# The order of the high and the low product in feature-major column tiles of a hybrid encoder block

## The chip, the cores and the metric

The kernel runs on one core of a Trainium2 chip. The metric is device time in microseconds (us) of one execution, lower is better. Engines are called as in the profile: PE (TensorE, its weight loads apart as PEld), DVE (VectorE), ACT (ScalarE), POOL (GpSimd), SP (which issues most of the DMAs).

## What is computed

One residual block over 256 tokens of width 2048, in float32: an RMS norm, one wide projection (`w_in`), stick-breaking attention with 16 heads and a Mamba-2 scan with 8 groups side by side, their gated sum through `w_out`, then a GeGLU MLP with a depthwise convolution ahead of the activation. Cut to what matters:

```python
h = rms_norm(x, norm_mix_pre)
q, k, v, z, xbc, dt, g_sb, g_ssd = jnp.split(h @ w_in, cuts, axis=-1)
o_sb = stick_breaking_attention(q, k, v)
xbc = silu(causal_dwconv(xbc, ssd_conv_w, ssd_conv_b))      # -> xs, bm, cm
y = ssd_scan(xs, softplus(dt + dt_bias), -exp(a_log), bm, cm)
y = rms_norm((y + xs * d_skip) * silu(z), ssd_norm)
x = x + rms_norm((sigmoid(g_sb) * (o_sb @ w_sb_proj) + sigmoid(g_ssd) * (y @ w_ssd_proj)) @ w_out, ...)
u = causal_dwconv(rms_norm(x, norm_ffn_pre) @ w_up, ffn_conv_w, ffn_conv_b)
x = x + rms_norm((gelu(gate) * val) @ w_down, norm_ffn_post)
```

Every large matrix product is made from three products of rounded halves: each float32 operand is split into a high half (`hi`, rounded to the fp32r type) and a low half (`lo`, the rest), and hi·hi, lo·hi and hi·lo are summed.

## The kernel before

**Weights.** All weights stream from HBM once, as 715 units of 128x1024. SP loads a unit into `raw` (5 buffers); `prep` splits it: ACT casts `whi` from `raw` (L63) and DVE subtracts `wlo` from both (L64), 5 buffers each. `unit()` (L95) hands out the next unit and keeps the splitting three units ahead.

**Two kinds of column tiles.** In token-major tiles (`tok_mm`, L136) activations are the weights of PE and each step is three products of 512 columns, `ps_z`, `ps_ssd`, `ps_fo` and others. In feature-major tiles a 128-wide column of the weight matrix is PE's stationary operand, and the activation chunk `act[:, k, :, :]` holds the high half of 256 tokens and then the low half. So one weight tile k of 16 needs two products into one PSUM bank `ps` of 512 columns: the high weights over both halves (512 columns, L112), and the low weights over the high half (256 columns, into the first 256 columns, L113). `feat_mm` (L115) runs 16 weight tiles for one bank, which is two units; `feat_mms` (L123) does the same for four or two banks side by side, four weight tiles at a time, where activations arrive late. Feature-major are `ps_first` (start), `ps_xs` and `ps_bc` (scan inputs, 6 tiles for each of 8 groups), `ps_qk` (32 tiles) and the up projection `ps_fg` and `ps_fv` (43 tiles each, after the first pair `ps_f0`).

**Taking a bank out.** `feat_sum` copies the second half of the bank with ACT (L133), and DVE adds the first half (L134). A convolution follows: for the scan `conv_silu` (DVE L314, ACT L315, three DVE steps L317, ACT's silu L318), for the MLP `conv3`.

**The scan of a group.** `ssd_work` is a generator whose steps `pump()` puts between PE's large products, during `ps_z` of the group and the next group's `ps_xs`: eight transposes `px` (L332), DVE's `xw` from them (L333), copies by ACT (L334), scalings by POOL (L336, L335), the decay matrix `mm` by DVE (L338), masked by POOL (L339), ACT's exponential (L347) and a copy of `pcb` to `xw` (L345), and then the product `po` (L353), which needs that copy.

**What sets the order.** Most of the order on each engine comes from a scheduler that places instructions when the program is built, by its own estimate of when their inputs are ready; only the first stage, the norm after `w_out` and the end are written out by hand (`manual_schedule`). So a change in when a bank counts as finished can move ACT's and DVE's instructions too.

Of the kernel before, what the change touches and what calls it, by code (L numbers as in the profile page):

```python
# [17 lines left out]
P = 128  # L18
T = 256
KT = 16  # L20
# [18 lines left out]
def block_kernel(ctx, tc, xT, xN, wts, vecs, rows, hvec, dskip, gain, out):  # L39


    nc = tc.nc
# [38 lines left out]
    def prep(parts=1):  # L81

        v = state["u"]
        state["u"] += 1
        if v not in raw_t:
            load(v)
        raw = raw_t.pop(v)
        hi = wspl.tile([P, 1024], F32R, tag="whi", name=f"whi{v}")
        lo = wspl.tile([P, 1024], F32R, tag="wlo", name=f"wlo{v}")
        spl_t[v] = (hi, lo)  # L90
        n = 1024 // parts
        for i in range(parts):
            w = slice(i * n, (i + 1) * n)
            split(hi[:, w], lo[:, w], raw[:, w])
            yield  # L95

    def unit(ahead=WBUFS - 2):

        u = state["at"]
        state["at"] += 1  # L100
        while state["u"] <= min(u + ahead, n_units - 1):
            for _ in prep():
                pass
        return spl_t.pop(u)

    def mm_bank(name):
        return pmm.tile([P, 512], F32, tag="mm", name=name)

    def feat_tile(ps, hi, lo, c, act, k, last):

        w = slice(c * P, (c + 1) * P)
        nc.tensor.matmul(ps, hi[:, w], act[:, k % 4, :, :].rearrange("p s t -> p (s t)"), start=(k == 0), stop=last)  # L112
        nc.tensor.matmul(ps[:, :T], lo[:, w], act[:, k % 4, 0, :], start=False, stop=last, skip_group_check=True)  # L113

    def feat_mm(acts, name):  # L115
        ps = mm_bank(name)
        for k in range(KT):
            if k % 8 == 0:
                hi, lo = unit()
            feat_tile(ps, hi, lo, k % 8, acts[k // 4], k, k == KT - 1)  # L120
        return ps

    def feat_mms(acts, pss):  # L123

        for kc in range(4):
            for i, ps in enumerate(pss):
                if i % 2 == 0:
                    hi, lo = unit()
                for k in range(4):
                    feat_tile(ps, hi, lo, 4 * (i % 2) + k, acts[kc], 4 * kc + k, 4 * kc + k == KT - 1)  # L130

    def feat_sum(ps, dst):
        nc.scalar.copy(dst, ps[:, T:])  # L133
# [2 lines left out]
    def tok_mm(acts, nk, name):  # L136

        pss = [mm_bank(f"{name}_{t}") for t in range(2)]
        for k in range(nk):
            if k % 2 == 0:  # L140
                hi, lo = unit()
            w = slice(k % 2 * 512, k % 2 * 512 + 512)
            for t in range(2):
                ah, al = (acts[k // 4][:, k % 4, s, t * P:(t + 1) * P] for s in range(2))
                nc.tensor.matmul(pss[t], ah, hi[:, w], start=(k == 0), stop=False)  # L145
                nc.tensor.matmul(pss[t], ah, lo[:, w], start=False, stop=False)  # L146
                nc.tensor.matmul(pss[t], al, hi[:, w], start=False, stop=(k == nk - 1))  # L147
            if k % 4 == 3:
                pump()
        return pss  # L150
# [155 lines left out]
    def conv_in(ps, ti):  # L306
        raw = tmp.tile([P, T], F32, tag="cv_raw", name=f"cvr{ti}", bufs=3)
        feat_sum(ps, raw)
        return raw
# [91 lines left out]
    first = [mm_bank(f"ps_first{i}") for i in range(3)]  # L401
    first.append(paux.tile([P, 512], F32, tag="aux", name="ps_first3"))
    feat_mms(a_ch, first)
    feat_sum(first[0][:64, :], dts[:64, 0, :])
    first = [None] + [conv_in(first[i], i - 1) for i in range(1, 4)]
    stats_x()
    for g in range(GROUPS):
        xf = []
        for j in range(4):
            xf.append(tmp.tile([P, T], F32, tag=f"xf{j}", name=f"xf{g}_{j}", bufs=1))  # L410
            if g == 0 and j < 3:
                continue
            ps = feat_mm(a_ch, f"ps_xs{g}_{j}")
            if g == 0:
                tok_to_bc(rstd_bc, rstd_tok, paux, "aux", "rx")
                bg.append(dt_work())
                for i in range(3):
                    conv_silu(first[i + 1], i, xf[i])
            conv_silu(conv_in(ps, 4 * g + j), 4 * g + j, xf[j])
            pump()  # L420
        bcs = []
        for j in range(2):
            ps = feat_mm(a_ch, f"ps_bc{g}_{j}")
            bcs.append(tmp.tile([P, T], F32, tag=f"bc{j}", name=f"bc{g}_{j}", bufs=1))
            conv_silu(conv_in(ps, 32 + 8 * j + g), 32 + 8 * j + g, bcs[j])
            pump()
        drain()
        csb = slot(F32, [8, T], f"csb{g}")
        nc.gpsimd.dma_start(csb, cs_dram[8 * g:8 * g + 8, :].partition_broadcast(P))
        xs = slot(F32, [2, 2, 512], f"xs{g}")  # L430
        bg.append(ssd_work(g, xf, bcs[0], bcs[1], xs, csb))
        pz = tok_mm(a_ch, KT, f"ps_z{g}")
        for t in range(2):
            nc.scalar.activation(xs[:, 0, t, :], pz[t], AF.Silu, scale=rstd_tok[:, t:t + 1])
# [12 lines left out]
    for n in range(4):  # L447
        ps = tok_mm(y_ch, 32, f"ps_ssd{n}")
# [69 lines left out]
    for hg in range(4):  # L518
        qk = slot(F32, [2, 4, T], f"qk{hg}")
        for i in range(2):  # L520
            for h in range(4):
                ps = feat_mm(a_ch, f"ps_qk{hg}_{i}_{h}")
                d = qk[:, i, h, :]
                feat_sum(ps, d)
                nc.vector.scalar_tensor_tensor(d, d, SCALE if i == 0 else 1.0, rstd_bc, op0=ALU.mult, op1=ALU.mult)
                pump()
        vt = slot(F32, [2, 512], f"v{hg}")
        pv = tok_mm(a_ch, KT, f"ps_v{hg}")
        for t in range(2):
            nc.scalar.activation(vt[:, t, :], pv[t], AF.Copy, scale=rstd_tok[:, t:t + 1])  # L530
        bg.append(attn_work(hg, qk, vt))
# [15 lines left out]
    for n in range(4):  # L547
        ps = tok_mm(o_ch, KT, f"ps_sb{n}")
# [59 lines left out]
    for n in range(4):  # L608
        ps = tok_mm(m_ch, KT, f"ps_mo{n}")
# [9 lines left out]
    with tc.manual_schedule(engines=ACT_DVE):  # L619
# [8 lines left out]
        for i in range(8 + lag):  # L628
            if i < 8:
                n, t = divmod(i, 2)  # L630
# [3 lines left out]
            if i >= lag:  # L634
                n, t = divmod(i - lag, 2)
# [43 lines left out]
    for j in range(FF_T):  # L679
        if j == 0:  # L680
            first = [mm_bank(f"ps_f0_{i}") for i in range(2)]
            feat_mms(h_ch, first)
            continue
        pg = feat_mm(h_ch, f"ps_fg{j}")
        pv = feat_mm(h_ch, f"ps_fv{j}")
        if j == 1:
            for t in range(2):
                nc.gpsimd.dma_start(x2_dram[t], xn[t])
            tok_to_bc(r2, n2.r, paux, "tp", "r2")
            ffn_out(0, *first)  # L690
        ffn_out(j, pg, pv)
# [11 lines left out]
    for n in range(4):  # L703
        gfo = tmp.tile([P, 512], F32, tag="gfo", name=f"gfo{n}")
        nc.gpsimd.dma_start(gfo, rows[2, blk(n)].partition_broadcast(P))
        ps = tok_mm(f_ch, FF_T, f"ps_fo{n}")
# [6 lines left out]
    with tc.manual_schedule(engines=ACT_DVE):  # L713
# [6 lines left out]
        for n in range(4):  # L720
            for t in range(2):
                parts = 2 if n == 3 and t == 1 else 1
                for i in range(parts):
                    w = slice(n * 512 + i * 256, (n + 1) * 512 - (parts - 1 - i) * 256)
# [84 lines left out]
```

## Time and profile before

| | |
|---|---|
| median of 3 runs | 2100.11 us (2099.76 to 2102.88) |
| the profiled execution | 2101.31 us |
| span of its trace | 2099.6 us |
| PE busy | 2072.1 us, 99% |
| weight loads (beside PE) | 1760.7 us, 84% |
| DVE / ACT / POOL busy | 1386.0 / 1156.9 / 152.3 us |
| DMA | 402.79 MB, mean 192 GB/s |

The span runs from the first to the last instruction in the trace; the time of the execution holds it and a little around it. PE is busy in all but a few places. A busy PE is not a PE at its peak: how long a product really holds PE is read from the distance of two starts, since a product's recorded length runs into the next one.

### The profile page before, as it was taken

How to read it: one execution, taken by the hardware profiler on the slowest of the kernel's cores; microseconds unless marked ns; L12 is line 12 of the kernel's file. 1: busy time of each engine (PE TensorE's matmuls, PEld its weight loads, DVE VectorE, ACT ScalarE, POOL GpSimd, SP SyncE). 2: the span in 40 equal slices, each digit the busy share in tenths (PEclk: the TensorE clock that was granted, in tenths of full speed). 3: DMA queues.
4: the chain of work that ended last, by engine and by line, in shares of the span. 5: the costliest groups of instructions: out<-in, count | busy, mean ns of one | idle time of the engine just before them, and what ended most of it. 6: DMA issues, size and time to landing. Idle time of an engine off the chain costs nothing.

```text
span 2099.6 us, 27950 instructions
## 1 busy us (share of the span) xinstructions
PE 2072.1 (99%) x10632; PEld 1760.7 (84%) x10632; DVE 1386.0 (66%) x1794; ACT 1156.9 (55%) x1542; POOL 152.3 (7%) x134
## 2 busy tenths in 40 slices
PE   9999999999999999999999999999999999999997
PEld 7788888888888888888888888788888888888886
DVE  6888877788544445555544566598878887854443
ACT  6767677667543334555556444475555555544442
POOL 0222102222000000000000021100000000000000
PEclk9999999999999999999999999999999999999999
DMA  8564565555555555555555746475555555565653
GB/s 297 194 205 160 190 205 186 176 199 179 187 197 192 192 194 186 180 171 171 170 172 185 274 161 210 141 250 191 189 190 190 189 189 190 191 232 202 195 193 109
DMA packets 109094, 402.79 MB, mean 192 GB/s; under 512 B 12416, under 2 KB 12672, under 8 KB 106656
## 3 DMA queue, kind: packets, MB, share of 16 engines
q1 hardware_dynamic: 104912, 380.07, 54.1%
q0 software_dynamic: 3328, 20.02, 2.7%
q8 instruction: 83, 1.36, 0.3%
q10 hardware_dynamic: 720, 0.93, 0.1%
q14 instruction: 51, 0.42, 0.1%
HBM read 396.71 MB, written 4.26 MB: 191 GB/s over the span
## 4 chain that ended last, share of the span: by engine, by line
PE 92%; POOL 2%; DVE 2%; issue 2%; DMA 1%; ACT 1%; SPq 0%; DVEq 0%; ACTq 0%; POOLq 0%
PE ps_fv L112 8%; PE ps_fg L112 8%; PE ps_qk L112 6%; PE ps_xs L112 5%; PE ps_fo L147 4%; PE ps_fo L145 4%; PE ps_fo L146 4%; PE ps_fg L113 4%; PE ps_fv L113 4%; PE ps_qk L113 3%; PE ps_ssd L147 3%; PE ps_ssd L145 3%; PE ps_ssd L146 3%; PE ps_xs L113 2%; PE ps_bc L112 2%; PE ps_z L146 2%
## 5 line engine op out<-in xcount | busy, mean ns | idle before, releaser
L64 DVE TENSOR_TENSOR wlo<-raw,whi 128x1024 fp32r<-128x1024 f32 (+1 forms) x715 | 905.1, 1270 | 601.2 <-ACT whi L63 600.6
L63 ACT CAST whi<-raw 128x1024 fp32r<-128x1024 f32 (+1 forms) x715 | 746.2, 1051 | 793.7 <-PE ps_fo L147 128.9
L112 PE MATMUL ps_fg<-h,whi 128*128 128x512 f32 x688 | 240.7, 394 | 0.0
L112 PE MATMUL ps_fv<-h,whi 128*128 128x512 f32 x688 | 240.6, 394 | 0.0
L113 PE MATMUL ps_fg<-h,wlo 128*128 128x256 f32 x688 | 190.6, 277 | 0.0
L113 PE MATMUL ps_fv<-h,wlo 128*128 128x256 f32 x688 | 190.6, 277 | 0.0
L112 PE MATMUL ps_qk<-a,whi 128*128 128x512 f32 x512 | 181.3, 398 | 0.0
L112 PE MATMUL ps_xs<-a,whi 128*128 128x512 f32 x464 | 162.9, 396 | 0.0
L112 PEld LDWEIGHTS ps_fv<-h,whi 128*128 128x128 f32 x688 | 129.0, 188 | 30.0
L112 PEld LDWEIGHTS ps_fg<-h,whi 128*128 128x128 f32 x688 | 129.0, 188 | 30.0
L113 PE MATMUL ps_qk<-a,wlo 128*128 128x256 f32 x512 | 143.5, 280 | 0.0
L145 PE MATMUL ps_fo<-whi,f 128*128 128x512 f32 x352 | 136.9, 389 | 0.0
L147 PE MATMUL ps_fo<-whi,f 128*128 128x512 f32 x352 | 136.9, 389 | 0.0
L146 PE MATMUL ps_fo<-wlo,f 128*128 128x512 f32 x352 | 136.9, 389 | 0.0
L113 PEld LDWEIGHTS ps_fg<-h,wlo 128*128 128x128 f32 x688 | 129.2, 188 | 0.0
L113 PEld LDWEIGHTS ps_fv<-h,wlo 128*128 128x128 f32 x688 | 129.2, 188 | 0.0
L113 PE MATMUL ps_xs<-a,wlo 128*128 128x256 f32 x464 | 129.0, 278 | 0.0
L112 PEld LDWEIGHTS ps_qk<-a,whi 128*128 128x128 f32 x512 | 96.1, 188 | 22.6
L145 PE MATMUL ps_z<-whi,a 128*128 128x512 f32 x256 | 103.7, 407 | 0.0
L112 PEld LDWEIGHTS ps_xs<-a,whi 128*128 128x128 f32 x464 | 87.1, 188 | 19.6
L146 PE MATMUL ps_z<-wlo,a 128*128 128x512 f32 x256 | 100.4, 392 | 1.0 <-DVE wlo L64 1.0
L147 PE MATMUL ps_z<-whi,a 128*128 128x512 f32 x256 | 100.1, 391 | 0.0
(282 smaller groups left out, 3832.5 us busy)
## 6 DMA issues: line engine op xcount, KB each, us to landing
raw<-wts SPq DMA_DIRECT2D x713, 512.0 KB, 3.8
csb<-cs_dram POOLq DMA_DIRECT2D x8, 1024.0 KB, 8.1
xt<-xN SPq DMA_DIRECT2D x2, 1024.0 KB, 10.6
csb<-gain POOLq DMA_DIRECT2D x8, 256.0 KB, 4.1
xn<-xN POOLq DMA_DIRECT2D x2, 1024.0 KB, 7.9
x_dram<-xn POOLq DMA_DIRECT2D x2, 1024.0 KB, 9.0
xe<-x_dram POOLq DMA_DIRECT2D x2, 1024.0 KB, 10.3
x<-xT SPq DMA_DIRECT2D x3, 512.0 KB, 9.2
```

What stands on the lines that cost most here:

```text
L63: nc.scalar.copy(hi, src)
L64: nc.vector.tensor_tensor(lo, src, hi.bitcast(F32), op=ALU.subtract)
L112: nc.tensor.matmul(ps, hi[:, w], act[:, k % 4, :, :].rearrange("p s t -> p (s t)"), start=(k == 0), stop=last)
L113: nc.tensor.matmul(ps[:, :T], lo[:, w], act[:, k % 4, 0, :], start=False, stop=last, skip_group_check=True)
L145: nc.tensor.matmul(pss[t], ah, hi[:, w], start=(k == 0), stop=False)
L146: nc.tensor.matmul(pss[t], ah, lo[:, w], start=False, stop=False)
L147: nc.tensor.matmul(pss[t], al, hi[:, w], start=False, stop=(k == nk - 1))
```

## The change

`feat_tile` and the loops around it are replaced by `feat_run`. It goes through a run of weight tiles (16 in `feat_mm`, 4 in `feat_mms`). In the first weight tile of a run the 512-column product with the high half still comes first; from the second on the 256-column product with the low half comes ahead of the 512-column product. So a run that was hi lo, hi lo, hi lo, ... is now hi lo, lo hi, lo hi, ..., and ends on a 512-column product. Number, size and operands of the products are the same.

```diff
-    def feat_tile(ps, hi, lo, c, act, k, last):
-        w = slice(c * P, (c + 1) * P)
-        nc.tensor.matmul(ps, hi[:, w], act[:, k % 4, :, :].rearrange("p s t -> p (s t)"), start=(k == 0), stop=last)
-        nc.tensor.matmul(ps[:, :T], lo[:, w], act[:, k % 4, 0, :], start=False, stop=last, skip_group_check=True)
+    def feat_run(ps, act, tiles, n, first, last):
+        for i, (hi, lo, k) in enumerate(tiles):
+            a = act(k)
+            for part in ("hi", "lo") if i == 0 else ("lo", "hi"):
+                end = last and i == n - 1
+                if part == "hi":
+                    nc.tensor.matmul(ps, hi, a.rearrange("p s t -> p (s t)"), start=first and i == 0, stop=end)
+                else:
+                    nc.tensor.matmul(ps[:, :T], lo, a[:, 0, :], start=False, stop=end, skip_group_check=True)
...
     def feat_mm(acts, name):
...
-            feat_tile(ps, hi, lo, k % 8, acts[k // 4], k, k == KT - 1)
+        feat_run(ps, lambda k: acts[k // 4][:, k % 4, :, :], tiles(), KT, True, True)
...
     def feat_mms(acts, pss):
...
-                for k in range(4):
-                    feat_tile(ps, hi, lo, 4 * (i % 2) + k, acts[kc], 4 * kc + k, 4 * kc + k == KT - 1)
+                feat_run(ps, lambda k: acts[kc][:, k, :, :], [(*w_tile(w, 4 * (i % 2) + k), k) for k in range(4)], 4, kc == 0, kc == 3)
```

The line numbers of the changed file are 5 to 12 higher: the two products are L117 and L119 there, `feat_sum` is L145 and L146, and later lines are 12 higher. In the rows of order below, numbers behind a name are buffer numbers.

PE, the beginning of the column tile `ps_fg41` of the up projection, before:

```order
L113 MATMUL ps_fv40_15637<-h3_11052,wlo613_15596 128x256
...
L112 MATMUL ps_fg41_15703<-h0_11049,whi614_15617 128x512
L113 MATMUL ps_fg41_15703<-h0_11049,wlo614_15618 128x256
L112 MATMUL ps_fg41_15703<-h0_11049,whi614_15617 128x512
L113 MATMUL ps_fg41_15703<-h0_11049,wlo614_15618 128x256
```

and now:

```order
L117 MATMUL ps_fv40_15637<-h3_11052,whi613_15595 128x512
...
L117 MATMUL ps_fg41_15703<-h0_11049,whi614_15617 128x512
L119 MATMUL ps_fg41_15703<-h0_11049,wlo614_15618 128x256 x2
L117 MATMUL ps_fg41_15703<-h0_11049,whi614_15617 128x512
L119 MATMUL ps_fg41_15703<-h0_11049,wlo614_15618 128x256
```

Two 256-column products now stand together at each beginning, and two 512-column products at each boundary between tiles. Everything else on PE, the transposes and products of the scan and of attention among them, has kept its place in the row.

DVE, in group 2 of the scan, from the bank of the group's last feature-major tile (`ps_bc2_1`, taken out to `cvr42`) to `xw2`, before:

```order
L64 TENSOR_TENSOR wlo58_1823<-raw58_1820,whi58_1822 128x1024
L134 TENSOR_TENSOR cvr42_1787<-cvr42_1787,ps_bc2_1_1741 128x256
L314 TENSOR_TENSOR cvr42_1787<-cvr42_1787,rstd_bc_218 128x256
L64 TENSOR_TENSOR wlo59_1868<-raw59_1865,whi59_1867 128x1024
L317 SCALAR_TENSOR_TENSOR cva42_1790<-cvr42_1787,vec_93,cva42_1790 128x255
L317 SCALAR_TENSOR_TENSOR cva42_1790<-cvr42_1787,vec_93,cva42_1790 128x254
L317 SCALAR_TENSOR_TENSOR cva42_1790<-cvr42_1787,vec_93,cva42_1790 128x253
L333 TENSOR_TENSOR xw2_1838<-px2_0_1840,dt_tok_220 128x512
```

and now:

```order
L146 TENSOR_TENSOR cvr42_1787<-cvr42_1787,ps_bc2_1_1741 128x256
L326 TENSOR_TENSOR cvr42_1787<-cvr42_1787,rstd_bc_218 128x256
L64 TENSOR_TENSOR wlo58_1823<-raw58_1820,whi58_1822 128x1024
L329 SCALAR_TENSOR_TENSOR cva42_1790<-cvr42_1787,vec_93,cva42_1790 128x255
L329 SCALAR_TENSOR_TENSOR cva42_1790<-cvr42_1787,vec_93,cva42_1790 128x254
L329 SCALAR_TENSOR_TENSOR cva42_1790<-cvr42_1787,vec_93,cva42_1790 128x253
L64 TENSOR_TENSOR wlo59_1868<-raw59_1865,whi59_1867 128x1024
L345 TENSOR_TENSOR xw2_1838<-px2_0_1840,dt_tok_220 128x512
```

The taking out of the bank and its convolution now stand one weight unit earlier than before. Groups 3 to 7 show the same pair of orders; group 1 had the second order before the change, and keeps it.

ACT at the same place, before:

```order
L63 CAST whi58_1822<-raw58_1820 128x1024
L318 ACTIVATE bc2_0_1730<-cva34_1734 128x256
L133 COPY cvr42_1787<-ps_bc2_1_1741 128x256
L63 CAST whi59_1867<-raw59_1865 128x1024
L315 ACTIVATE cva42_1790<-cvr42_1787,vec_93 128x256
L63 CAST whi60_1885<-raw60_1883 128x1024
L318 ACTIVATE bc2_1_1786<-cva42_1790 128x256
L334 COPY xs2_1799<-px2_0_1840 128x512
```

and now:

```order
L330 ACTIVATE bc2_0_1730<-cva34_1734 128x256
L145 COPY cvr42_1787<-ps_bc2_1_1741 128x256
L63 CAST whi58_1822<-raw58_1820 128x1024
L327 ACTIVATE cva42_1790<-cvr42_1787,vec_93 128x256
L63 CAST whi59_1867<-raw59_1865 128x1024
L330 ACTIVATE bc2_1_1786<-cva42_1790 128x256
L63 CAST whi60_1885<-raw60_1883 128x1024
L346 COPY xs2_1799<-px2_0_1840 128x512
```

Here too the convolution's steps stand one weight cast earlier. ACT's list also has 18 fewer table loads (63 instead of 81), three for each of the groups 1 to 6, in the stage of the next group's `ps_xs`.

DVE in group 0, after `rstd_bc` (the reciprocal norm, which all convolutions of the scan need), before:

```order
L254 COPY rstd_bc_218<-rx_ps_449 128x256
L64 TENSOR_TENSOR wlo14_533<-raw14_530,whi14_532 128x1024
L314 TENSOR_TENSOR cvr0_379<-cvr0_379,rstd_bc_218 128x256
...
L317 SCALAR_TENSOR_TENSOR cva1_461<-cvr1_382,vec_93,cva1_461 128x253
L264 TENSOR_SCALAR dts_226<-dts_226,hv_195 64x256
L64 TENSOR_TENSOR wlo15_567<-raw15_564,whi15_566 128x1024
L317 SCALAR_TENSOR_TENSOR cva2_468<-cvr2_385,vec_93,cva2_468 128x255
```

and now:

```order
L266 COPY rstd_bc_218<-rx_ps_449 128x256
L326 TENSOR_TENSOR cvr0_379<-cvr0_379,rstd_bc_218 128x256
...
L329 SCALAR_TENSOR_TENSOR cva1_461<-cvr1_382,vec_93,cva1_461 128x253
L276 TENSOR_SCALAR dts_226<-dts_226,hv_195 64x256
L64 TENSOR_TENSOR wlo14_533<-raw14_530,whi14_532 128x1024
L64 TENSOR_TENSOR wlo15_567<-raw15_564,whi15_566 128x1024
L329 SCALAR_TENSOR_TENSOR cva2_468<-cvr2_385,vec_93,cva2_468 128x255
```

The split of unit 14 has moved behind the eleven instructions that follow `rstd_bc`. SP's and POOL's lists, the DMAs among them, are the same as before.

## Rows read from the trace of the kernel before

**Rows 1.** The page: the span, and busy time, share of the span and instructions of each engine.

```profile
span 2099.6 us, 27950 instructions
...
PE 2072.1 (99%) x10632; PEld 1760.7 (84%) x10632; DVE 1386.0 (66%) x1794; ACT 1156.9 (55%) x1542; POOL 152.3 (7%) x134
```

**Rows 2.** The waits of PE, the five longest of eight: who waited, for whom, us in total, times, the longest.

```profile
PE po L353 <- ACT xw L345: 3.7, 6, 0.7
PE pth L385 <- DVE mog L632: 2.9, 1, 2.9
PE ps_first L112 <- DVE a L197: 2.9, 2, 2.1
PE po L353 <- POOL xw L336: 2.4, 1, 2.4
...
PE ps_z L146 <- DVE wlo L64: 1.0, 1, 1.0
```

**Rows 3.** PE in order of time in the up projection, across the boundary of two column tiles: start, recorded length, instruction.

```profile
1502.74 0.39 PE L112 MATMUL ps_fv<-h,whi 128*128 128x512 f32 x1
...
1503.32 0.28 PE L113 MATMUL ps_fv<-h,wlo 128*128 128x256 f32 x1
1503.44 0.39 PE L112 MATMUL ps_fg<-h,whi 128*128 128x512 f32 x1
...
1503.78 0.40 PE L112 MATMUL ps_fg<-h,whi 128*128 128x512 f32 x1
```

**Rows 4.** PE in order of time in the first `ps_qk` tiles; between the two rows stand two other pairs.

```profile
805.17 0.40 PE L112 MATMUL ps_qk<-a,whi 128*128 128x512 f32 x1
...
806.23 0.40 PE L112 MATMUL ps_qk<-a,whi 128*128 128x512 f32 x1
```

**Rows 5.** The page's costliest groups: two of the 512-column products, with count, busy time and mean ns of one.

```profile
L112 PE MATMUL ps_fg<-h,whi 128*128 128x512 f32 x688 | 240.7, 394 | 0.0
...
L112 PE MATMUL ps_qk<-a,whi 128*128 128x512 f32 x512 | 181.3, 398 | 0.0
```

**Rows 6.** Group 1 of the scan, during its `ps_z`, in order of time, of PE, then DVE, then POOL: start, length, instruction, and the idle time before it with what ended it.

```profile
126.19 1.04 PE L332 MATMUL px<-ident,xf 128*128 128x128 f32 x8
...
138.92 0.67 PE L353 MATMUL po<-xw 128*128 128x512 f32 x1
...
125.06 1.22 DVE L64 TENSOR_TENSOR wlo<-raw,whi 128x1024 fp32r<-128x1024 f32 x1
126.83 1.29 DVE L333 TENSOR_TENSOR xw<-px,dt_tok 128x512 f32<-128x512 f32 x2 [0.55 <-PE px L332]
...
127.61 1.03 POOL L336 TENSOR_TENSOR xw<-xw,dec 128x512 f32<-128x512 f32 x1 [39.58 <-DVE xw L333]
```

**Rows 7.** Group 2 at the same place, of PE, DVE, ACT and POOL.

```profile
188.57 1.04 PE L332 MATMUL px<-ident,xf 128*128 128x128 f32 x8
...
201.79 0.67 PE L353 MATMUL po<-xw 128*128 128x512 f32 x1 [0.60 <-ACT xw L345]
...
187.13 1.23 DVE L64 TENSOR_TENSOR wlo<-raw,whi 128x1024 fp32r<-128x1024 f32 x1 [0.69 <-ACT whi L63]
188.27 1.52 DVE L317 SCALAR_TENSOR_TENSOR cva<-cvr,vec,cva 128x255 f32<-128x255 f32 x3
189.70 1.28 DVE L333 TENSOR_TENSOR xw<-px,dt_tok 128x512 f32<-128x512 f32 x2
...
188.77 1.05 ACT L63 CAST whi<-raw 128x1024 fp32r<-128x1024 f32 x1 [1.18 <-PE ps_z L147]
...
190.42 1.19 ACT L334 COPY xs<-px 128x512 f32<-128x512 f32 x2
...
190.48 1.03 POOL L336 TENSOR_TENSOR xw<-xw,dec 128x512 f32<-128x512 f32 x1 [43.58 <-DVE xw L333]
```

**Rows 8.** Group 7 at the same place, PE alone; groups 3 to 6 stand between.

```profile
502.90 1.04 PE L332 MATMUL px<-ident,xf 128*128 128x128 f32 x8
...
516.12 0.67 PE L353 MATMUL po<-xw 128*128 128x512 f32 x1 [0.59 <-ACT xw L345]
```

**Rows 9.** Group 0, from `rstd_bc` to the wait in `ps_z`: one row of PE, then DVE, then ACT, in order of time.

```profile
58.73 0.50 PE L146 MATMUL ps_z<-wlo,a 128*128 128x512 f32 x1 [1.00 <-DVE wlo L64]
...
41.28 1.23 DVE L64 TENSOR_TENSOR wlo<-raw,whi 128x1024 fp32r<-128x1024 f32 x1
42.42 1.09 DVE L314 TENSOR_TENSOR cvr<-cvr,rstd_bc 128x256 f32<-128x256 f32 x3
...
46.39 1.21 DVE L64 TENSOR_TENSOR wlo<-raw,whi 128x1024 fp32r<-128x1024 f32 x1
48.43 0.48 DVE L317 SCALAR_TENSOR_TENSOR cva<-cvr,vec,cva 128x255 f32<-128x255 f32 x1 [0.84 <-ACT cva L315]
...
57.46 1.22 DVE L64 TENSOR_TENSOR wlo<-raw,whi 128x1024 fp32r<-128x1024 f32 x1
...
45.89 1.28 ACT L318 ACT_TABLE_LOAD   x1 [0.97 <-DVE cva L317]
...
47.81 0.59 ACT L315 ACTIVATE cva<-cvr,vec 128x256 f32<-128x256 f32 x1
```

**Rows 10.** Busy time of each engine in two stretches, with PE's granted clock as a share of full speed (after POOL).

```profile
9.00:15.20 6.20, 5.25 (x16) 4.48 (x17) 4.79 (x9) 5.41 (x10) 0.00 (x0) 0.50 1.03 417
1353.50:1357.00 3.50, 3.46 (x19) 3.21 (x17) 3.50 (x7) 2.27 (x4) 0.00 (x0) 0.51 0.00 0
```

More of the change, by code (lines that the diff above doesn't have):

```diff
@@ L107, in mm_bank, with w_tile, tiles @@
         return pmm.tile([P, 512], F32, tag="mm", name=name)
-    def feat_tile(ps, hi, lo, c, act, k, last):
-        w = slice(c * P, (c + 1) * P)
-        nc.tensor.matmul(ps, hi[:, w], act[:, k % 4, :, :].rearrange("p s t -> p (s t)"), start=(k == 0), stop=last)
-        nc.tensor.matmul(ps[:, :T], lo[:, w], act[:, k % 4, 0, :], start=False, stop=last, skip_group_check=True)
+    def feat_run(ps, act, tiles, n, first, last):
[7 more added lines that the diff above has]
+                    nc.tensor.matmul(ps[:, :T], lo, a[:, 0, :], start=False, stop=end, skip_group_check=True)
+    def w_tile(w, c):
+        return tuple(x[:, c * P:(c + 1) * P] for x in w)
     def feat_mm(acts, name):
         ps = mm_bank(name)
-        for k in range(KT):
-            if k % 8 == 0:
-                hi, lo = unit()
-            feat_tile(ps, hi, lo, k % 8, acts[k // 4], k, k == KT - 1)
+        def tiles():
+            for k in range(KT):
+                if k % 8 == 0:
+                    w = unit()
+                yield *w_tile(w, k % 8), k
+        feat_run(ps, lambda k: acts[k // 4][:, k % 4, :, :], tiles(), KT, True, True)
         return ps
@@ L127, in feat_mms @@
                 if i % 2 == 0:
-                    hi, lo = unit()
-                for k in range(4):
-                    feat_tile(ps, hi, lo, 4 * (i % 2) + k, acts[kc], 4 * kc + k, 4 * kc + k == KT - 1)
+                    w = unit()
+                feat_run(ps, lambda k: acts[kc][:, k, :, :], [(*w_tile(w, 4 * (i % 2) + k), k) for k in range(4)], 4, kc == 0, kc == 3)
     def feat_sum(ps, dst):
```

## The prediction

> **What bounds the kernel now.** I read the page's busy shares first, then PE's waits, then PE in order of time, then DVE and ACT around each wait. PE is busy for 2072.1 of 2099.6 us and DVE, the next engine, for 66% [rows 1]. So the time moves in two ways only: by how fast PE goes through its row of products, or by places where PE stands still.
>
> For the rate, the distance of starts counts. In the up projection three pairs of a 512- and a 256-column product take 1503.78 - 1502.74 = 1.04 us, 0.347 us a pair, and the tile boundary that lies inside (`ps_fv` to `ps_fg`) adds nothing [rows 3]. In the first `ps_qk` tiles three pairs of the same shape take 1.06 us, 0.353 us a pair [rows 4]; the page's mean lengths of the 512-column product, 394 and 398 ns, differ in the same direction [rows 5]. So identical instructions run in two rhythms 1.06 - 1.04 = 0.02 us per three pairs apart, that is 6.7 ns a pair (a difference of rounded rows, good to some ns). Each lasts through whole stages.
>
> PE's listed waits are few, and three bear on the change: `po` on ACT's copy 3.7 us in six pieces, `po` on POOL 2.4 us once, `ps_z` on DVE's `wlo` 1.0 us once [rows 2]. The two others in that list lie at the start and between attention and the gate, on norm and gate steps whose row the change leaves alone.
>
> **Part 1, the products.** Removed and added: nothing. There are (43 + 43) x 16 = 1376 pairs in the up projection (688 of them `ps_fg` [rows 5]), 512 in `ps_qk`, 48 x 16 = 768 in the scan's inputs, and some 64 more at the start and in the first up pair, 2720 in all. Each run of 16 keeps 16 products of either size. After each product stands another that needs new weights, before and now; what is new are two neighbours of a kind at each end of a run (256 after 256, 512 after 512). If a product holds PE for its columns and a fixed share, the sum of a run is the same, whatever the order: 0. No row of before shows 256 after 256 in this form, so the cost is bounded by the nearest rows, the two rhythms: from -6.7 ns to +6.7 ns a pair, where a stage could still change over. I take 0, because rows 3 are nearest: there a boundary, where 256 follows 512 and another bank begins, costs nothing that can be read. Weights: the low half is now wanted 0.23 us or so earlier in a run (second, instead of fourth, in line at the second weight tile), but no wait of a feature-major product on `wlo` is in the list [rows 2], and splitting is three units ahead, so 0.
>
> How the trace bears on a rule here: the 1.04 us for three pairs stay above the pure columns, 3 x 768 / 2.4 = 960 ns [rows 3], at the higher of the clock's two levels. The Trainium skill ("TensorE: Matmul & The Clock Gate", Part 2, Back-to-back issue gap) gives N/2.4 + 2.5 ns a product, by which a pair is an estimated 325 ns in any order, and its Part 2, Step-by-step, says that weight loads do not take bandwidth from a running product. By it no order of neighbours could cost anything, and both rivals on the rhythm would be void; rows 3 and 4, at 347 and 353 ns for the same instructions, do not agree with one fixed figure, so the measurement decides and these rivals keep their chances.
>
> **Part 2, a bank's end.** The last product of a bank is now the one of 512 columns, which writes both halves, where ACT could before start on the second half while the 256-column product ran (by its columns 256 / 2.4 = 107 ns; with its share of the overhead about 0.12 us). So ACT's copy comes 0.12 us later, at each of 163 or so banks. I cost that at nothing: `px` needs `xf` only after the group's last tiles, `ps_z` covers it, and the up projection's convolutions are a tile behind. If this cover were gone everywhere it would be 163 x 0.12 = 19.6 us. The `whi` buffer comes free 0.12 us later too, once per unit, with four more behind it. ACT's 18 dropped table loads (1.28 us each [rows 9]) free ACT, which is at 55% [rows 1]: 0 on the path. SP's and POOL's rows are the same, so no DMA moves in its queue.
>
> **Part 3, groups 2 to 7 of the scan.** This is where PE stands still. In group 1 `px` starts at 126.19 and `po` at 138.92, 12.73 us later, with no wait written at it [rows 6]; in group 2 it is 201.79 - 188.57 = 13.22, with 0.60 of wait on ACT's copy [rows 7]; in group 7 516.12 - 502.90 = 13.22, with 0.59 [rows 8]. PE's row is the same in all of them, so the 0.49 is lost time. Back along the chain: ACT's copy stands behind the exponential of the matrix that POOL masks, and POOL does that after its `xw`; POOL starts 127.61 in group 1 and 190.48 in group 2, and from there to `po` it is 11.31 us in both (138.92 - 127.61, 201.79 - 190.48). So the delay arises ahead of POOL, and passes on one for one. DVE makes `xw` from `px`: in group 1 at 126.83, 0.64 after `px`, having waited for PE [rows 6]; in group 2 at 189.70, 1.13 after `px`, because three steps L317 of the last convolution, from 188.27, still stand ahead and run until 189.79 [rows 7]. 1.13 - 0.64 = 0.49 again.
>
> The change gives groups 2 to 7 the order that group 1 had: L314 and L317 of the last convolution stand one weight split earlier on DVE, and on ACT the copies and L315 one cast earlier (ACT's cast at 188.77, after an idle 1.18, stands between them [rows 7]). What is moved behind, the split of a later unit (1.23 us), is wanted three units on. So I expect 0.49 x 6 = 2.94 us less. Bounds: 0, if something else is late instead (DVE's split of 1.22 us, which in group 1 stands directly ahead of `xw` at 125.06 and ends 0.55 before it [rows 6]), and 3.7, all the wait of the row [rows 2]. I take 2.9 to 3.0, because group 1 shows the very order. Next late after it is `px` itself, that is PE.
>
> **Part 4, group 0.** After `rstd_bc` DVE splits unit 14 first (41.28, 1.23 us), then does L314 and what follows at 42.42 [rows 9]. Now the split goes behind eleven instructions, so these start 1.14 us earlier. ACT's table load at 45.89, which waited 0.97 for DVE's L317, comes at 44.75; behind it `cva` (47.81 + 0.59) ends at 47.26 instead of 48.40. DVE will do split 14 at about 45.25 and split 15 at 46.39 as before, until about 47.5; so its idle 0.84 before 48.43 [rows 9] goes, and its dense list after it starts about 0.9 us earlier. Split 14 is wanted only by `ps_z` of group 0, some 4 us after its new end. In that list stands split 16 (57.46), on which PE waits 1.00 at 58.73 [rows 9]; 0.9 to 1.0 of it goes. The rest of group 0's chain (`px`, POOL, the 2.4 us wait of `po` [rows 2]) hangs on the same list and moves with it, not more than PE does. I take -1.0; bounds 0 (something else on the list takes the time) and -1.16 (1.14 moved, with rounding).
>
> **The sum.** 0 + 0 - 3.0 - 1.0 = -4.0 us. Against the profiled execution, 2101.31 - 4.0 = 2097.3; the median of the three runs, 2100.11, is 1.2 below that execution, so **2096.1 us** (-0.19%). From run to run about 0.2%, 4.2 us, can be told from no change, so the forecast stands just at that line (2095.9).
>
> One thing can shift all cases: the granted clock. It stands at 0.50 for a stretch at the start (9.0 to 15.2) and 0.51 at 1353.5 to 1357.0 [rows 10], that is the lower level; at half speed 3.5 us of PE's work holds 1.75 us of loss, and a stretch that begins or ends elsewhere could bring or take so much.
>
> **The rivals.**
>
> *A: no gain.* The wait comes back elsewhere: PE reaches the next gate, the exponential or POOL, as much earlier as it saved, and waits there, or the mended order loses its lead to a later cast. Then 2100.1. For it: `po` of group 0 waits for POOL anyway [rows 2]. Against it: group 1 has no wait with this order [rows 6].
>
> *B: slower.* The up projection loses its rhythm. Its 1376 pairs are in the quicker one now [rows 3]; what sets a rhythm is not in the rows, but it seems to be taken on entry into a stage and kept, so a boundary with two equal neighbours, which comes 86 times, may throw it into the other. Price: 1376 x 6.7 ns = 9.2 us, so 2096.1 + 9.2 = 2105.3, or +5.2 on the time before (+0.25%). It decides against the forecast as soon as more than 4.0 / 0.0067, some 600 pairs, go over, and is past the measurable from about 1230. For it: two rhythms exist, with the same instructions [rows 3, 4]. Against it: old boundaries also change bank and weights, and leave the rhythm alone.
>
> *C: more gain.* The same, with the other sign: `ps_qk`'s 512 pairs fall into the quicker rhythm: 512 x 6.7 ns = 3.4 us, 2092.7.
>
> *D: the change does not do what it says.* Each run could still be built with the low product behind. The built order shows it in front; this has no chance left worth a number.
>
> **How the numbers follow.** Forecast 0.57, with 2094.3 to 2097.6 as its own range (gains of 5.8 to 2.5: the bounds of parts 3 and 4, and the clock); half of it lies past 2095.9. A 0.15, same. B 0.14, of which 0.12 beyond 2104.3 and 0.02 in between. C 0.14, faster. So faster 0.27 + 0.14 = 0.41, same 0.30 + 0.15 + 0.02 = 0.47, slower 0.12. For 8 in 10 the range holds the forecast and A whole, and C down to 2092.3; it leaves out B's full price and a few hundredths at the ends: 2092.3 to 2101.0.
>
> **What would show it.** Right: `px` to `po` 12.7 us in groups 2 to 7 as in group 1, the six waits of `po` on ACT gone, `ps_z` on `wlo` down to 0.1 us or less, 0.347 us a pair in `ps_fg` and 0.353 in `ps_qk`. Wrong: waits of the same sum at another name (A); three `ps_fg` pairs in 1.06 us (B), or three `ps_qk` pairs in 1.04 (C); a first wait of feature-major products on weights; or a new low stretch of the granted clock.

## The result, and the profile after

| | before | changed |
|---|---|---|
| median of 6 runs | 2101.93 us (2099.76 to 2102.88) | 2108.42 us (2106.56 to 2111.14) |
| the profiled execution | 2101.31 us | 2106.56 us |
| span of its trace | 2099.6 us | 2104.7 us |

The ratio is 1.0033, with a 95% interval of 1.002 to 1.0046: slower by 0.33%, where -0.19% was forecast. The page of the changed kernel, for [rows 1, 5]:

```profile
span 2104.7 us, 27952 instructions
...
PE 2082.2 (99%) x10632; PEld 1765.5 (84%) x10632; DVE 1394.4 (66%) x1794; ACT 1137.9 (54%) x1524; POOL 159.5 (8%) x134
...
L117 PE MATMUL ps_fg<-h,whi 128*128 128x512 f32 x688 | 246.9, 398 | 0.0
...
L117 PE MATMUL ps_qk<-a,whi 128*128 128x512 f32 x512 | 181.0, 399 | 0.0
```

PE does the same 10632 products and is busy 10.1 us longer; the mean length of the up projection's product went from 394 to 398 ns, to that of `ps_qk`, whose length moved by 1 ns only. So PE did not wait more, it went slower. The waits of PE, for [rows 2]:

```profile
PE pth L397 <- DVE mog L644: 2.9, 1, 2.9
PE po L365 <- POOL xw L348: 2.4, 1, 2.4
PE ps_first L119 <- ACT a L208: 1.6, 1, 1.6
PE wake L183 <- DVE ones L180: 1.1, 1, 1.1
PE ptm L397 <- DVE gat L564: 0.4, 1, 0.4
PE po L365 <- ACT xw L357: 0.2, 1, 0.2
```

The six waits of `po` on ACT have shrunk from 3.7 us to one of 0.2, and `ps_z` no longer waits for `wlo` at all: the waits that were to go are gone, and none has come in their place. PE in order of time across a tile boundary of the up projection, for [rows 3]:

```profile
1502.27 0.40 PE L117 MATMUL ps_fv<-h,whi 128*128 128x512 f32 x1
1502.51 0.39 PE L117 MATMUL ps_fg<-h,whi 128*128 128x512 f32 x1
1502.73 0.40 PE L119 MATMUL ps_fg<-h,wlo 128*128 128x256 f32 x2
1502.96 0.40 PE L117 MATMUL ps_fg<-h,whi 128*128 128x512 f32 x1
...
1503.32 0.40 PE L117 MATMUL ps_fg<-h,whi 128*128 128x512 f32 x1
...
1504.38 0.40 PE L117 MATMUL ps_fg<-h,whi 128*128 128x512 f32 x1
```

The boundary itself is cheap: the two 512-column products start 0.24 and 0.22 us before what follows, the two 256-column ones take 0.23 together. But behind it, where low and high alternate as before the change, three pairs take 1504.38 - 1503.32 = 1.06 us instead of 1.04. That is the rhythm of [rows 4]. How far this reaches is read from the number of products in one window of 450 us inside the up projection, of before and then of the changed kernel (stretch, its length, PE busy with its products, granted clock, DMA):

```profile
1390.00:1840.00 450.00, 450.00 (x2598) 1.00 0.58 191
```

```profile
1390.00:1840.00 450.00, 450.00 (x2552) 1.00 0.58 189
```

2 x 450 / 2598 = 0.3464 us a pair before, 2 x 450 / 2552 = 0.3527 now, at a granted clock of 1.00 in both: 6.2 ns more, over the whole stage. It holds 42 pairs of banks behind the norm's product, 1344 pairs: 8.4 us.

Set beside each other product for product, the changed kernel's trace is 1.3 us ahead where the first `ps_z` begins (the clock's first low stretch was shorter: 0.91 granted in the first 20 us against 0.83), 3.1 us ahead behind `po` of group 7, still 3.1 ahead at the up projection, and 5.2 behind at the end.

The scan, group 2 and then PE in group 7, for [rows 7, 8], PE, DVE and POOL in order of time:

```profile
184.18 1.52 DVE L329 SCALAR_TENSOR_TENSOR cva<-cvr,vec,cva 128x255 f32<-128x255 f32 x3
...
185.62 1.22 DVE L64 TENSOR_TENSOR wlo<-raw,whi 128x1024 fp32r<-128x1024 f32 x1
...
186.94 1.04 PE L344 MATMUL px<-ident,xf 128*128 128x128 f32 x8
...
187.57 1.29 DVE L345 TENSOR_TENSOR xw<-px,dt_tok 128x512 f32<-128x512 f32 x2 [0.74 <-PE px L344]
188.36 1.03 POOL L348 TENSOR_TENSOR xw<-xw,dec 128x512 f32<-128x512 f32 x1 [43.36 <-DVE xw L345]
...
199.68 1.10 PE L365 MATMUL po<-xw 128*128 128x512 f32 x2
...
500.29 1.04 PE L344 MATMUL px<-ident,xf 128*128 128x128 f32 x8
...
513.03 1.10 PE L365 MATMUL po<-xw 128*128 128x512 f32 x2
```

From `px` to `po` it is 199.68 - 186.94 = 12.74 and 513.03 - 500.29 = 12.74 us, where it was 13.22 [rows 7, 8], and 12.73 in group 1 [rows 6]. The steps L329 now end before the split at 185.62, DVE waits 0.74 for `px`, and `xw` starts 0.63 after it, not 1.13. Group 0, DVE and one row of PE, for [rows 9]:

```profile
39.65 0.42 DVE L266 COPY rstd_bc<-rx_ps 128x256 f32<-128x256 f32 x1
40.11 1.10 DVE L326 TENSOR_TENSOR cvr<-cvr,rstd_bc 128x256 f32<-128x256 f32 x3
...
44.08 2.35 DVE L64 TENSOR_TENSOR wlo<-raw,whi 128x1024 fp32r<-128x1024 f32 x2
46.35 0.48 DVE L329 SCALAR_TENSOR_TENSOR cva<-cvr,vec,cva 128x255 f32<-128x255 f32 x1
...
55.16 1.21 DVE L64 TENSOR_TENSOR wlo<-raw,whi 128x1024 fp32r<-128x1024 f32 x1
...
56.42 0.50 PE L158 MATMUL ps_z<-wlo,a 128*128 128x512 f32 x1
```

The splits of units 14 and 15 stand in a row, DVE no longer idles before the L329 step behind them, and the product that wanted unit 16 starts without a wait.

### The profile page after: what moved, and what is told of

It is laid out like the page before. It is cut to its first block, busy times and chain, and to the rows that moved or that the text cites. A ratio compares the mean times of both kernels' runs of the same rounds, so it can differ in the third digit from the quotient of the medians.

```text
span 2104.7 us, 27952 instructions
## 1 busy us (share of the span) xinstructions
PE 2082.2 (99%) x10632; PEld 1765.5 (84%) x10632; DVE 1394.4 (66%) x1794; ACT 1137.9 (54%) x1524; POOL 159.5 (8%) x134
## 4 chain that ended last, share of the span: by engine, by line
PE 96%; DMA 1%; DVE 1%; issue 1%; ACT 0%; POOL 0%; SPq 0%; DVEq 0%; ACTq 0%; POOLq 0%
PE ps_fv L117 8%; PE ps_fg L117 8%; PE ps_qk L117 6%; PE ps_xs L117 5%; PE ps_fg L119 4%; PE ps_fv L119 4%; PE ps_fo L159 4%; PE ps_fo L157 4%; PE ps_fo L158 4%; PE ps_qk L119 3%; PE ps_bc L117 3%; PE ps_ssd L158 3%; PE ps_ssd L159 3%; PE ps_ssd L157 3%; PE ps_z L158 3%; PE ps_z L157 3%
## 5 line engine op out<-in xcount | busy, mean ns | idle before, releaser
L117 PE MATMUL ps_fg<-h,whi 128*128 128x512 f32 x688 | 246.9, 398 | 0.0
L117 PE MATMUL ps_fv<-h,whi 128*128 128x512 f32 x688 | 246.8, 398 | 0.0
L119 PE MATMUL ps_fg<-h,wlo 128*128 128x256 f32 x688 | 186.2, 281 | 0.0
L119 PE MATMUL ps_fv<-h,wlo 128*128 128x256 f32 x688 | 186.2, 281 | 0.0
L117 PE MATMUL ps_qk<-a,whi 128*128 128x512 f32 x512 | 181.0, 399 | 0.0
L117 PE MATMUL ps_xs<-a,whi 128*128 128x512 f32 x464 | 163.4, 397 | 0.0
L117 PEld LDWEIGHTS ps_fg<-h,whi 128*128 128x128 f32 x688 | 129.4, 188 | 28.2
L117 PEld LDWEIGHTS ps_fv<-h,whi 128*128 128x128 f32 x688 | 129.4, 188 | 28.2
L119 PE MATMUL ps_qk<-a,wlo 128*128 128x256 f32 x512 | 138.1, 280 | 0.0
L119 PEld LDWEIGHTS ps_fv<-h,wlo 128*128 128x128 f32 x688 | 130.0, 189 | 3.7
L119 PEld LDWEIGHTS ps_fg<-h,wlo 128*128 128x128 f32 x688 | 130.0, 189 | 3.7
L119 PE MATMUL ps_xs<-a,wlo 128*128 128x256 f32 x464 | 125.0, 280 | 0.0
L117 PEld LDWEIGHTS ps_qk<-a,whi 128*128 128x128 f32 x512 | 95.1, 188 | 20.8
L117 PEld LDWEIGHTS ps_xs<-a,whi 128*128 128x128 f32 x464 | 86.0, 188 | 17.8
## 6 DMA issues: line engine op xcount, KB each, us to landing
xt<-xN SPq DMA_DIRECT2D x2, 1024.0 KB, 10.1
```

The costliest lines, as they stand in the source:

```text
L117: nc.tensor.matmul(ps, hi, a.rearrange("p s t -> p (s t)"), start=first and i == 0, stop=end)
L119: nc.tensor.matmul(ps[:, :T], lo, a[:, 0, :], start=False, stop=end, skip_group_check=True)
```

## The experiments

All kernels here choose the order within a weight tile by one function, `parts(name, i, n)`, with the bank's name, the weight tile's place i in its run and the run's length n. The kernel before is `("hi", "lo")` for all; the changed one has `("lo", "hi")` from i = 1 on. Nothing else differs, so each edit is shown as this function's. Where the low product is the first of a bank it carries the start flag. The products in the window from 1390 to 1840 us tell the rhythm of the up projection: about 2598 if quick, about 2550 if slow.

| kernel | time, us | ratio to before, 95% | products in the window |
|---|---|---|---|
| before | 2101.9 | | 2598 |
| changed | 2108.4 | 1.0033 (1.002 to 1.0046) | 2552 |
| low first everywhere | 2097.29 | 0.9979 (0.9971 to 0.9988) | 2598 |
| changed, up projection old | 2099.96 | 0.9989 (0.9981 to 0.9998) | 2598 |
| only the last tile, up projection | 2110.14 (one run) | | 2549 |
| only the middle tiles, up projection | 2106.28 (one run) | | 2575 |
| two banks | 2104.16 (one run) | | 2582 |
| low first in the scan's inputs | 2097.37 | 0.9979 (0.997 to 0.9989) | 2597 |
| the last tile of each group | 2098.92 | 0.999 (0.9981 to 0.9998) | 2598 |
| low first, one `ps_qk` bank turned | 2098.19 (one run) | | |
| blocks of five | 2110.06 (one run) | | 2577 |

**Low first everywhere.**

```diff
-    return ("hi", "lo") if i == 0 else ("lo", "hi")
+    return ("lo", "hi")
```

> Low product first in every weight tile, the first of a run too, so that 256- and 512-column products alternate without exception and no two equal ones stand together; a bank still ends on the 512-column product, and DVE and ACT keep the changed kernel's order but for two or three neighbours. Theory K (two equal neighbours at each run boundary throw PE into the slower rhythm, which then stays): three pairs of the up projection take 1.04 us again, the gains of the scan stay, so 2101.9 - 3.1 (what the changed kernel is ahead when it enters the up projection) = 2099 us, a few us either way for the entries into the other stages. Rival L (low ahead of high, or the later end of the bank, costs by itself): three pairs take 1.06 us as in the changed kernel, 2107 to 2109.

Measured 2097.29 us, faster than both kernels. PE across a boundary of the up projection:

```profile
1499.12 0.39 PE L119 MATMUL ps_fv<-h,whi 128*128 128x512 f32 x1
...
1499.82 0.39 PE L119 MATMUL ps_fv<-h,whi 128*128 128x512 f32 x1
1500.05 0.28 PE L121 MATMUL ps_fg<-h,wlo 128*128 128x256 f32 x1
1500.16 0.39 PE L119 MATMUL ps_fg<-h,whi 128*128 128x512 f32 x1
```

1500.16 - 1499.12 = 1.04 us for three pairs. The bank ends on the high product and low stands ahead of high in every tile, as in the changed kernel (in all but the first there); only the equal neighbours are gone. So neither the later end of a bank nor low ahead of high costs by itself: L falls, K stands.

**The changed kernel with the old order in the up projection.**

```diff
-    return ("hi", "lo") if i == 0 else ("lo", "hi")
+    return ("hi", "lo") if i == 0 or name[:5] in ("ps_fg", "ps_fv") else ("lo", "hi")
```

> The changed kernel, but the tiles ps_fg and ps_fv of the up projection in the old order (high, low); the rest of the change stays. Theory K and rival L alike: the loss lies in the up projection alone (8.3 us by the traces), so 2108.4 - 8.3 = 2100 us, under the kernel before by what group 0 and groups 2 to 7 of the scan save, less what the scan inputs lose (3.1 us by the traces: 2098.8 against 2101.9). If the loss is not local (rhythm taken over from an earlier stage, or contention from elsewhere), the up projection stays at 1.06 us for three pairs and the time near 2108.

2099.96 us and 2598 products: the loss lies in the up projection, 2108.42 - 2099.96 = 8.5 us of it, and what is left of the change is a gain of 0.11%.

**Only the last tile, and only the middle tiles, of the up projection's banks.** Both start from the kernel before.

```diff
-    return ("hi", "lo")
+    return ("lo", "hi") if i == n - 1 and name[:5] in ("ps_fg", "ps_fv") else ("hi", "lo")
```

> The kernel before, with the two products swapped in the last weight tile alone of each ps_fg and ps_fv: low after low one pair ahead of the end, high after high at the boundary; 15 of 16 tiles keep high ahead of low. Theory K: equal neighbours are enough, three pairs 1.06 us, 2101.9 + 8.6 = 2110. Rival L in its first form (low ahead of high costs): one tile of 16, +0.5 us, 2102.5. L in its second form (the bank ends later): the same as K, 2110.

2110.14 us, 2549 products: swapping one tile of 16 does all the harm, so the price has nothing to do with the number of swapped pairs.

```diff
-    return ("hi", "lo")
+    return ("lo", "hi") if 0 < i < n - 1 and name[:5] in ("ps_fg", "ps_fv") else ("hi", "lo")
```

> The kernel before, with the products swapped in weight tiles 2 to 15 of 16 of each ps_fg and ps_fv, not in the first and the last: the bank ends on the low product as before, DVE's list is that of before, low after low stands at the start and high after high one tile ahead of the end. Theory K: 1.06 us for three pairs, 2110. L in its first form (low ahead of high): 14 of 16, about 2109 to 2110 too. L in its second form (the bank ends later): no loss, 2101.9.

2106.28 us, 2575 products: half the loss, which neither theory had foreseen. The first products of five banks in a row:

```profile
1449.43 0.40 PE L119 MATMUL ps_fg<-h,whi 128*128 128x512 f32 x1
...
1455.08 0.39 PE L119 MATMUL ps_fv<-h,whi 128*128 128x512 f32 x1
...
1460.63 0.40 PE L119 MATMUL ps_fg<-h,whi 128*128 128x512 f32 x1
...
1466.27 0.39 PE L119 MATMUL ps_fv<-h,whi 128*128 128x512 f32 x1
...
1471.82 0.40 PE L119 MATMUL ps_fg<-h,whi 128*128 128x512 f32 x1
```

The steps are 5.65, 5.55, 5.64, 5.55 us: `ps_fg` slow, `ps_fv` quick, in turn. The bank's end is that of before here, and so is DVE's list; so neither is needed for the loss.

**Two banks alone.** From the kernel before.

```diff
-    return ("hi", "lo")
+    return ("lo", "hi") if 0 < i < n - 1 and name in ("ps_fg10", "ps_fg30") else ("hi", "lo")
```

> The kernel before, with the products of weight tiles 2 to 15 swapped in two banks of the up projection alone, ps_fg10 and ps_fg30. The rows of the run in which the middle tiles of all banks were swapped show slow and quick banks in turn, so theory F is that such a bank's two pairs of equal neighbours (256 after 256, 512 after 512) turn the rhythm over, and that it then stays by itself. F: quick up to ps_fg10, slow at 0.353 us a pair from there to ps_fg30 (40 banks of 16 pairs, 640 x 6.7 ns = 4.3 us), quick again after it: 2101.9 + 4.3 = 2106.2. Rival D, the disturbance dies away: only the banks beside the two are slow, at most 0.5 us, 2102.4. Rival S, equal neighbours always set the slow one: slow from ps_fg10 to the end, 66 banks, 2101.9 + 7.1 = 2109.

2104.16 us. Two stretches of the up projection, between the two banks and behind the second (columns as in the windows above, with PEld, DVE, ACT and POOL behind PE):

```profile
1480.00:1690.00 210.00, 210.00 (x1214) 185.15 (x1213) 169.26 (x266) 120.12 (x190) 0.00 (x0) 1.00 0.58 190
1700.00:1840.00 140.00, 140.00 (x794) 121.45 (x793) 110.34 (x175) 78.75 (x124) 0.00 (x0) 1.00 0.59 185
```

2 x 210 / 1214 = 0.346 us a pair, then 2 x 140 / 794 = 0.353. The first disturbed bank left the rate as it was; the second, with the same instructions, brought the slow rhythm, and it stayed for all 27 banks behind. Yet the first did change something that the trace shows: the mean recorded length of the 512-column products of `ps_fg` is 394 ns from 1400 to 1465 us, 391 from 1480 to 1690 and 399 from 1700 to 1840, that of the 256-column ones 277, 280 and 281. So the quick rhythm has two kinds here, and the two disturbed banks did not meet the same one. F was wrong in its first half (a bank does not always turn the rate over) and right in its second (the rhythm stays), D is ruled out, and S holds at one of two places.

**Blocks of five.** From the kernel before.

```diff
-    return ("hi", "lo")
+    return ("lo", "hi") if name[:5] in ("ps_fg", "ps_fv") and int(name[5:]) // 5 % 2 else ("hi", "lo")
```

> The kernel before, with the low product first in every weight tile of ps_fg and ps_fv in blocks of five pairs of banks (5 to 9, 15 to 19, 25 to 29, 35 to 39), the old order in the others. Equal neighbours then stand alone, each kind four times: 256 after 256 where a low-first block begins, 512 after 512 where it ends, ten banks apart, and everywhere else 512 and 256 alternate. Theory K (equal neighbours set the rhythm, which then stays): the rhythm can change at these eight boundaries and nowhere else; within a block all ten banks have one rhythm. If 512 after 512 is the one that leaves the slow rhythm: 19 pairs of banks slow, 608 x 6.7 ns = 4.1 us, 2106; if 256 after 256 is: 20 pairs of banks, 4.3 us, 2106, in the other blocks; if each depends on the state it meets, fewer. Rival: low ahead of high is itself slow: the low-first blocks slow from their first to their last bank, whatever the neighbours; rival drift: changes inside blocks.

The time, 2110.06 us, holds a long low stretch of the granted clock (0.74 on the mean of 80 to 100 us, where the kernel before has 1.00; at most 0.26 x 20 = 5.2 us), so it is not compared; the up projection is read by itself. The first product of each block:

```profile
1419.48 0.28 PE L121 MATMUL ps_fg<-h,wlo 128*128 128x256 f32 x1
...
1474.94 0.40 PE L119 MATMUL ps_fg<-h,whi 128*128 128x512 f32 x1
...
1530.42 0.28 PE L121 MATMUL ps_fg<-h,wlo 128*128 128x256 f32 x1
...
1585.89 0.39 PE L119 MATMUL ps_fg<-h,whi 128*128 128x512 f32 x1
...
1642.41 0.28 PE L121 MATMUL ps_fg<-h,wlo 128*128 128x256 f32 x1
...
1698.95 0.40 PE L119 MATMUL ps_fg<-h,whi 128*128 128x512 f32 x1
...
1755.47 0.28 PE L121 MATMUL ps_fg<-h,wlo 128*128 128x256 f32 x1
...
1810.95 0.39 PE L119 MATMUL ps_fg<-h,whi 128*128 128x512 f32 x1
...
1850.52 0.40 PE L119 MATMUL ps_fv<-h,whi 128*128 128x512 f32 x1
```

Ten banks of 16 pairs each take 55.46, 55.48, 55.47, 56.52, 56.54, 56.52 and 55.48 us: quick blocks are at 0.3467 us a pair, slow ones at 0.3533, and no block lies in between. Low-first blocks (those that begin with L121) are quick three times and slow once, so the order in itself is cleared. 256 after 256 left a quick rhythm quick twice, a slow one slow once, and turned a slow one quick once; 512 after 512 left one quick, turned one slow and left one slow; the last, at 1810.95, turned a quick one slow too, since the seven banks behind it, up to the last row, take (1850.52 - 1810.95) / 112 = 0.3533 us a pair.

So neither kind of neighbours has an outcome of its own. But the two kinds of the quick rhythm tell the outcomes apart. The 512-column products of `ps_fg` from 1480 to 1525, from 1535 to 1580 and from 1590 to 1640 us, one stretch in each of three blocks in a row (behind the count stand busy us, then mean ns):

```profile
L119 PE MATMUL ps_fg<-h,whi 128*128 128x512 f32 x66 | 23.1, 391 | 0.0
...
L119 PE MATMUL ps_fg<-h,whi 128*128 128x512 f32 x67 | 23.5, 394 | 0.0
...
L119 PE MATMUL ps_fg<-h,whi 128*128 128x512 f32 x69 | 24.6, 399 | 0.0
```

All stretches read in this way, ahead of the first block and then block by block:

| from, us | ahead of it stands | mean of the 512-column products, ns | rhythm |
|---|---|---|---|
| 1390 | | 394 | quick |
| 1419.48 | 256 after 256 | 391 | quick |
| 1474.94 | 512 after 512 | 391 | quick |
| 1530.42 | 256 after 256 | 394 | quick |
| 1585.89 | 512 after 512 | 399 | slow |
| 1642.41 | 256 after 256 | 399 | slow |
| 1698.95 | 512 after 512 | 399 | slow |
| 1755.47 | 256 after 256 | 394 | quick |
| 1810.95 | 512 after 512 | 399 | slow |

From a quick rhythm, 256 after 256 changes the one kind into the other, and 512 after 512 leaves 391 as it is and turns 394 slow. The run with two disturbed banks agrees, taking its two pairs in each bank in turn: 394, by 256 after 256 to 391 (the mean inside `ps_fg10`), which 512 after 512 leaves; then 391, by 256 after 256 to 394 (the mean inside `ps_fg30`), which 512 after 512 turns slow. In these two runs that fits all nine disturbances that meet a quick rhythm. It was read from them afterwards, and no run was made to test it. Three meet the slow one: 512 after 512 left it slow, and 256 after 256 left it slow once and led out of it once, with nothing in these means to tell the two apart.

**Low first in the scan's inputs alone**, and **the last tile of each group alone**, both from the kernel before: where do the gains come from?

```diff
-    return ("hi", "lo")
+    return ("lo", "hi") if name[:5] in ("ps_xs", "ps_bc") else ("hi", "lo")
```

> Low product first in every weight tile of ps_xs and ps_bc (no equal neighbours inside a run of tiles), the old order everywhere else. If what the low-first kernel gained is the scan's order on DVE and ACT (group 0 0.9, groups 2 to 7 0.45 each by its trace): 2101.9 - 0.9 - 6 x 0.45 = 2098.3, the up projection at 1.04 us for three pairs. Rival: the gain came from the quicker rhythm in ps_qk (most of the 0.9 us that the low-first trace gains after the scan) and at the start, and the scan's is taken back later: 2101 or more.

2097.37 us: within what can be told, all that the low-first kernel has. The rival's 2101 falls: the scan alone brings the time. Its premise holds in part, though. Set beside the kernel before product for product, the low-first trace is 2.5 us ahead where `ps_qk` begins and 3.8 where it ends; the trace of this kernel gains nothing there. The two times do not show that difference.

```diff
-    return ("hi", "lo")
+    return ("lo", "hi") if i == n - 1 and name[:5] == "ps_bc" and name[-1] == "1" else ("hi", "lo")
```

> The kernel before, with the two products swapped in the last weight tile alone of each ps_bc tile that ends a group (8 of 2720 pairs). On DVE only the splits of two weight units in each of groups 2 to 7 move behind the taking out of that bank and its convolution; ACT's copies move likewise, its table loads stay 81. If that order is the whole cause of the 0.5 us in groups 2 to 7: px to po 12.7 us in all of them, 2101.9 - 6 x 0.49 = 2098.9, and group 0 keeps its 1.0 us wait. Rival: the gain needs the other moves too (table loads, the order of ps_xs): no change, 2101.9.

2098.92 us, as expected. Two of PE's waits in it:

```profile
PE ps_z L160 <- DVE wlo L64: 1.0, 1, 1.0
...
PE po L367 <- ACT xw L359: 0.2, 1, 0.2
```

`po`'s six waits are gone and group 0's wait is left, with 8 swapped pairs of 2704. So the order on DVE and ACT around one bank is the whole cause of the gain in groups 2 to 7; the changed table loads and the other moves are not needed for it.

**Low first, with one `ps_qk` bank turned.**

```diff
-    return ("lo", "hi")
+    return ("hi", "lo") if 0 < i < n - 1 and name == "ps_qk0_0_0" else ("lo", "hi")
```

> The low-first kernel, with the high product first in weight tiles 2 to 15 of the first ps_qk bank alone (512 after 512 at its start, 256 after 256 at its end). The eight banks of that stretch run at 0.353 us a pair in the low-first kernel. If such a bank turns the rhythm over in both directions: 0.347 us a pair in the seven banks behind it, 7 x 16 x 6.7 ns = 0.75 us less in that stretch. Rival: slow is the rhythm that equal neighbours leave behind whatever was before: 0.353 us in all eight, no gain.

229 products from 790 to 830 us (the end of that bank and those behind it), against 228 in the low-first kernel: about 0.35 us a pair in both, no gain. The 512-column products behind that bank have a mean of 399 ns (791.5 to 829 us), that of the slow rhythm. Here the disturbance left slow slow, which is against F again.

## Why the prediction was wrong

**The step that failed** is in part 1: "I take 0, because rows 3 are nearest: there a boundary, where 256 follows 512 and another bank begins, costs nothing that can be read". The bound of +6.7 ns a pair was the right value, over the whole up projection: 6.2 ns by the windows, 8.4 us. Rows 3 showed that a change of bank and weights is harmless; they could say nothing about 256 after 256 and 512 after 512, which no row of before held, and the argument that a product holds PE for its columns and a fixed share was contradicted by [rows 3, 4] already: two rhythms with the same instructions mean that PE carries a state from product to product. A change that puts a new pattern into a stage where that state decides should have had far more than 0.14: 86 boundaries are 86 chances to disturb it. The order could only lose there, since the stage was in the quick rhythm, and of the kind (394 ns) that 512 after 512 turned slow in three cases of three.

**Rival B** is what happened, with its mechanism (an equal pair at the boundary throws the stage out of its rhythm, and it stays out), its place and nearly its price (9.2 forecast, 8.4 measured). It had a chance of 0.14. Not foreseen: it also took the scan's input tiles. `px` of groups 2 and 7 are 502.90 - 188.57 = 314.33 us apart before [rows 7, 8] and 500.29 - 186.94 = 313.35 now: 0.98 less, where five shorter stretches to `po` give 5 x 0.48 = 2.4; so some 1.4 us, 0.3 a group, went back to slower `ps_xs` and `ps_bc` tiles. The kernel with low first in these tiles keeps them quick: that is a part of its lead over the second experiment (2097.37 against 2099.96).

**Rival C** did not come: the mean of `ps_qk` went from 398 to 399 ns. Its premise, that each rhythm "lasts through whole stages", was a misreading: in the kernel before, the 512-column products of `ps_qk` have a mean of 399 ns from 789 to 833 us and of 391 from 875 to 885, and by the distances of their starts 9 of its 32 banks were quick already. So its price was at most 23 x 16 x 6.7 ns = 2.5 us, not 3.4.

**Part 2** was right: no wait of a bank's copy appeared, and the run with low first everywhere, whose banks end late too, shows it in its time. (The feature-major pairs are 2704 and the banks 169, not 2720 and 163; nothing in the sum hangs on it.) **Part 3** was right in mechanism and size: 12.74 against the 12.73 of group 1, 0.47 to 0.49 us in each of six groups, and the swap of 8 pairs alone brought 2.7 us of 2.9. **Part 4** was right: the wait of 1.00 us is gone; the run that leaves this order as it was has it still.

**The rule** weighed in part 1 (the Trainium skill, "TensorE: Matmul & The Clock Gate", Part 2, Back-to-back issue gap) gives N/2.4 + 2.5 ns as the isolated gap of a product, from its columns alone, so that no order of products could matter. It does not agree with these runs: 2598 against 2552 products in the same window, with the same products and granted clock.

Without the equal neighbours the sum would have stood: -4.0 us was forecast, and low first in every tile measured 2097.3 - 2101.9 = -4.6. That it comes so near is in part luck, since the trace of that kernel holds 1.3 us won in `ps_qk`, which the sum had at nothing.

**Open** stays what in PE the slow rhythm and the two kinds of the quick one are, why they last, and when a disturbance leads out of the slow one. The runs show where the state can change and, for a quick rhythm, which way it went; not how it is set.

## What to carry to other kernels

Where the same instructions run at two rates in one trace, as here, PE carries a state, and a reordering must be priced at the difference of the two over the whole stage behind it, not at the reordered place. Look at the mean recorded length of a product as well as at the rate: 391 and 394 ns went with the same rate here, and answered the same disturbance differently. Keep a strictly alternating pattern alternating across boundaries too: here moving the swap into the first tile as well turned +0.33% into -0.21%. And a small change in when a scheduler believes a result is ready can be worth more than the change itself: 8 swapped pairs gave most of the gain.

## What the hardware showed that was not expected

- In the up projection, a product stream that alternates 512 and 256 columns, with new weights for each, has two lasting rhythms at a granted clock of 1.00: 55.47 and 56.53 us for 160 pairs. No undisturbed block lay in between, and each lasted until the next two equal neighbours: at the longest followed behind a single disturbed bank, the slow one for 27 banks, some 150 us, and the quick one for 39, some 217 us.
- The quick rhythm has two kinds with the same rate and different recorded lengths: 391 and 280 ns for the two products (the low-first kernel), or 394 and 277 (the kernel before). 256 after 256 changed one into the other each time (four of four in the two runs above).
- So the outcome of one and the same disturbance differs: 512 after 512 left the quick rhythm alone at 1474.94, where it was of the 391 kind, and ended it at 1585.89 and 1810.95, where it was of the 394 kind.
